# A list schedule that models the port pair of VectorE and GpSimd, and picks engines without a discount

## Chip, cores and metric

One Trainium2 chip, one core. The metric is the device time of one execution in microseconds (us); lower is better. In the profile PE is TensorE, DVE is VectorE, ACT is ScalarE, POOL is GpSimd, SP is the queue that issues the DMAs.

## What is computed

A two-layer decoder trunk over 1024 tokens of width 1024, in float32. Each layer is a residual step:

```python
h = rms_norm(x, ln_g[layer]); u = h @ w_in[layer]          # one wide projection
# even layer: latent attention | compressed + selected + window attention | memory attention
# odd layer:  attention over the 256 best keys of an index score | mLSTM (chunked) | memory attention
mix = concat([y1 * silu(gate1), y2 * silu(gate2), y_m * silu(gate_m)])
x = x + mix @ w_out[layer]
```

Every attention is scores, mask, softmax over the keys, and a weighted sum of the values, for 4 or 8 heads.

## The kernel before

The work is tiled by 128 rows (eight tiles of tokens). Products are made in halves: a float32 operand is split into a high half in 16 bits (a cast) and a low half (the operand minus its high half), and three matmuls take the place of one. So each weight page `wr` (128x1024) is multiplied by a gain in place, cast to the high part of `wl`, and the low part of `wl` is `wr` minus the high part. Likewise each page of exponentials `P` that goes through a DMA transpose is cast into `PS` and has its low half subtracted (`u_split`). `nm` is the negated row maximum of a score tile, to which a constant is added; `cf` is a factor per head; `ms` is a mean square whose root is taken on GpSimd by a power operation.

The program is not written in order. `Recorder.add` records each instruction with its dependencies and a price in ns (`cost_of`). `Recorder.places` gives each instruction a place by the segment it belongs to (the table `SEG`). `Recorder.order` is a greedy list schedule: of the engines T, V, S, G (TensorE, VectorE, ScalarE, GpSimd) and Q (the DMA queue) it takes, again and again, the one whose next instruction could start first by the prices and by `latency`, and issues it. What comes out is one fixed sequence for each engine; the semaphores follow from the data, and no planned time goes into the program.

Some instructions may run on more than one engine (`Recorder.flex`): casts and scalings made by `copy` on V or S, elementwise operations of two tensors made by `tt` and `sub` on V or G. `elsewhere` decides for those, with the alternatives' prices weighted by `PRICE`:

```python
fin = {x: max(te[x], ready(o, x), shared(o, x), room) + alt[3] * (1 + PRICE[x]) for x, alt in o.alts.items()}
return min(fin.values()) < fin[e]
```

`te` is when the engine ends what it was last given. `shared` keeps an engine off a tile or bank of PSUM that another engine still touches. The prices that matter here, for m elements in a partition: V, two tensors, 1.042 m + 69; V, one tensor in SBUF, 0.525 m + 65; G, two tensors, 1.886 m + 148 with a 16-bit result and 2.104 m + 148 with a 32-bit one; S, 0.8333 m + 94 from SBUF.

Of the kernel before, what the change touches and what calls it, by code (L numbers as in the profile page):

```python
# [14 lines left out]
OP = mybir.AluOpType  # L15
# [9 lines left out]
PRICE = {"V": 1.12, "S": 1.2, "G": -0.64}  # L25
BANKED = ("B",)
_BASE = np.zeros(8 << 20, np.uint8)
_BASE0 = _BASE.__array_interface__["data"][0]

class VTile:  # L30
    """a tile that gets its place when the first instruction that touches it is issued"""
# [18 lines left out]
class View:  # L50
    """a view of a VTile: shape and extent now, the access pattern when it is issued"""
# [60 lines left out]
    def box(self):  # L112
        """partition and byte extent (p0, p1, b0, b1)"""
# [30 lines left out]
class Op:  # L144
    __slots__ = ("eng", "alts", "deps", "users", "cost", "tiles", "key", "seg", "ldw", "idx", "ndep", "end", "where", "name", "real", "start", "banks")
# [12 lines left out]
class Recorder:  # L158
    """records instructions, orders them by a list schedule over the engines, and issues them"""
# [7 lines left out]
    @contextmanager  # L167
    def segment(self, name, t0, t1):
        """instructions recorded inside take their places in the program from t0 to t1"""
        old, self.seg = self.seg, self.segs.setdefault(name, [t0, t1, 0.0])  # L170
        yield
        self.seg = old

    def flex(self, *alts):
        """alternatives (engine, method, args, keywords) for one instruction; the schedule takes one"""
        o = self.add(*alts[0])
        for eng, meth, args, kw in alts[1:]:
            outs, ins = self.split(args, kw)
            o.alts[eng] = (meth, args, kw, cost_of(eng, meth, outs, ins, args, kw))
        return o  # L180
# [9 lines left out]
    def add(self, eng, meth, args, kw):  # L190
# [28 lines left out]
        o.alts = {eng: (meth, args, kw, o.cost)}  # L219
        o.ldw = 0.0 if eng != "Q" else max(1220.0, 395 + o.cost) if kw.get("transpose") else PLAIN  # L220
# [4 lines left out]
        o.key = self.seg[2]  # L225
        o.where = None
# [3 lines left out]
    # ---------------------------------------------------------------- list schedule  # L230
    def places(self):
        """the program: instructions by place, work of the tensor engine ahead of each, first and last place of each tile"""
# [3 lines left out]
        for o in ops:  # L236
            t0, t1, w = o.seg
            o.key = t0 + (t1 - t0) * o.key / max(w, 1e-9)
# [54 lines left out]
    def order(self, window=6183873, dma_window=39829):  # L293
# [28 lines left out]

        def shared(o, e):
            """when the engines that touched the tiles of o first, or its banks last, let engine e at them"""
            t = 0.0
            for v in o.tiles:
                if v in first and first[v][0] != e:
                    t = max(t, first[v][1] + latency(first[v][0], e))
# [6 lines left out]
        def elsewhere(p, e):  # L335
            """whether another engine would finish the instruction at p well before e would, the engines' time at its price"""
# [13 lines left out]
        def clock(st, cost):  # L350
            """time of an instruction of the tensor engine, whose clock halves after a window with little work"""
# [16 lines left out]
        def fits(v, p, now):  # L368
            """(time, first slot) of the best free place for a tile of the instruction at p, or None; a pair of banks is kept for the next
            tile that needs one"""  # L370
# [15 lines left out]
        def alloc(p, now):  # L386
            """earliest time for the tiles that the instruction at p brings up, or None"""
# [14 lines left out]
        while len(out) < n:  # L402
# [100 lines left out]
            else:  # L503
                o.end = te[e] = st + (clock(st, o.cost) if e == "T" else o.cost)
            changed = False
# [43 lines left out]

def cost_of(eng, meth, outs, ins, args, kw):  # L550
    """nanoseconds an engine is held"""
    if meth.startswith("dma"):
# [7 lines left out]
        return a.size * a.itemsize / (360.0 if run >= 512 else 180.0)  # L560
# [35 lines left out]
def latency(a, b):  # L596
    """from the end of an instruction on engine a to the start of one on engine b that needs it"""
# [69 lines left out]
class Trunk:  # L667
# [64 lines left out]
    def sub(self, out, a, b, scale=1.0, engs="VG"):  # L732
        """out = a * scale - b"""
# [21 lines left out]
    # ------------------------------------------------------------------ constants  # L755
# [27 lines left out]
    def setup_late(self):  # L783
# [30 lines left out]
        # gains of keys without rotation go to the queries; a power of two balances queries and keys  # L814
# [64 lines left out]
    def rope(self, u, C, Sn, a, b, out):  # L879
        """u, a, b, out: [128, h, d]; C, Sn: [128, d]"""  # L880
# [7 lines left out]
    def split_rows(self, u, name, k=2, dup=1, dt=H):  # L888
        """u: [128, h, d] fp32; [128, h, k, d]: hi, lo (k = 2), hi, lo, lo, hi (k = 4) or hi, hi, lo, lo (dup = 2)"""
# [20 lines left out]
    def turn(self, out, in_):  # L910
        """out [128, n, rows] = in_ [rows, 128 * n] transposed, 128 columns at a time"""
        self.Q.dma_start(out, in_, transpose=True)

    def flip(self, src, dt=H):
        """transposes split rows src (list of [128 or less, 128]) into one psum bank"""
# [8 lines left out]
    # ------------------------------------------------------------------ normalised, transposed, split rows  # L924
    def norm_T(self, xt, tag):
        """rows of xt over their root mean square, times 1024: halves hi and lo, transposed"""
# [14 lines left out]
    # ------------------------------------------------------------------ weights  # L941
    def load_w(self, parts, nk, gain=None, fuse=False):
        """parts: list of dram AP [nk*128, n]; last: list over k of (hi [128, n], lo [128, n]) of the rows times gain times a power of
        two, and [128, 2]: what takes their products with rows times 1024 back, and half of it"""
# [1484 lines left out]
```

## Time and profile before

| | |
|---|---|
| median of 3 runs | 1698.34 us |
| lowest, highest | 1695.55 us, 1702.73 us |
| span of the profiled execution | 1695.3 us |
| instructions | 30,499 |
| matmuls | 10,407 |
| mean granted clock of TensorE | 0.949 |

The profiled execution has no time of its own beside its span of 1695.3 us; the median of the timed runs is 3.0 us above that span. An engine's busy time counts an instruction from start to end, and that includes the time in which it stood still after its start.

### The profile page before, as it was taken

How to read it: one execution, taken by the hardware profiler on the slowest of the kernel's cores; microseconds unless marked ns; L12 is line 12 of the kernel's file. 1: busy time of each engine (PE TensorE's matmuls, PEld its weight loads, DVE VectorE, ACT ScalarE, POOL GpSimd, SP SyncE). 2: the span in 40 equal slices, each digit the busy share in tenths (PEclk: the TensorE clock that was granted, in tenths of full speed). 3: DMA queues.
4: the chain of work that ended last, by engine and by line, in shares of the span. 5: the costliest groups of instructions: out<-in, count | busy, mean ns of one | idle time of the engine just before them, and what ended most of it. 6: DMA issues, size and time to landing. Idle time of an engine off the chain costs nothing. (4 is left out here: it accounts for less than half of the span.)

```text
span 1695.3 us, 30499 instructions
## 1 busy us (share of the span) xinstructions
PE 1420.5 (84%) x10407; PEld 795.2 (47%) x10407; DVE 1494.5 (88%) x3574; ACT 937.2 (55%) x2282; POOL 967.6 (57%) x982
## 2 busy tenths in 40 slices
PE   4889978888788877868888798788996788999888
PEld 1334434445566654544555354333442345556454
DVE  8864699999988998898888989989999799999894
ACT  5521545345666675555664357697965544355541
POOL 3563479888756566566565653423148667645461
PEclk9899989999999999979999899999998788899999
DMA  9804512237577778867996240021242036579997
GB/s 280 212 22 107 190 50 87 89 102 150 110 130 128 169 154 232 199 118 162 219 226 144 57 139 15 16 91 32 85 131 67 30 75 164 141 173 200 236 220 171
DMA packets 441853, 225.52 MB, mean 133 GB/s; under 512 B 378080, under 2 KB 404320, under 8 KB 441696
## 3 DMA queue, kind: packets, MB, share of 16 engines
q1 hardware_dynamic: 441696, 223.57, 55.7%
q8 instruction: 81, 1.33, 0.3%
q14 instruction: 76, 0.62, 0.1%
HBM read 83.61 MB, written 46.66 MB: 77 GB/s over the span
## 5 line engine op out<-in xcount | busy, mean ns | idle before, releaser
L542 PE MATMUL psum<-wl,hT 128*128 128x512 f16 (+3 forms) x2880 | 707.8, 382 | 40.4 <-POOL wl L542 9.1
L542 PEld LDWEIGHTS <-hT 128*128 128x128 f16 x2880 | 286.4, 101 | 354.4 <-issue 91.1
L542 POOL TENSOR_TENSOR PS<-P,PS 128x512 f16<-128x512 f32 (+6 forms) x153 | 216.7, 1418 | 122.3 <-DVE PS L542 54.3
L542 PE MATMUL psum<-wl,oT 128*128 128x512 f16 x960 | 273.2, 384 | 9.8 <-DMA oT<-osp 2.4
L542 PEld LDWEIGHTS <-PT 128*128 128x128 f16 x3792 | 235.3, 102 | 93.9 <-DMA PT<-PS 35.0
L542 ACT ACTIVATE P<-psum,nm 128x256 f32<-128x256 f32 (+8 forms) x336 | 191.8, 580 | 135.8 <-POOL nm L542 45.6
L542 POOL TENSOR_TENSOR wl<-wr,wl 128x1024 f16<-128x1024 f32 (+4 forms) x77 | 180.2, 2347 | 118.1 <-DVE wl L542 70.7
L542 PE MATMUL psum<-nv,PT 128*128 128x64 f16 x1584 | 189.1, 195 | 22.1 <-DVE PT L542 11.4
L542 POOL TENSOR_TENSOR ms<-ms,nhalf 128x4 f32<-128x4 f32 (+3 forms) x105 | 121.5, 1165 | 132.9 <-DVE ms L542 115.1
L542 ACT ACTIVATE tkj<-tkj 128x512 bf16<-128x512 bf16 (+5 forms) x192 | 149.5, 780 | 73.4 <-DVE tkj L542 50.1
L542 DVE TENSOR_REDUCE nm<-psum 128x2 f32<-128x512 f32 (+8 forms) x216 | 162.5, 763 | 15.5 <-PE psum L542 14.8
L542 PEld LDWEIGHTS <-oT 128*128 128x128 f16 x960 | 93.9, 99 | 104.8 <-issue 12.6
L542 PE MATMUL psum<-cst,P 128*128 128x128 f32 x502 | 106.6, 300 | 21.4 <-ACT P L542 11.5
L542 PEld LDWEIGHTS <-qf 128*128 128x128 f16 x832 | 78.2, 100 | 64.1 <-issue 29.0
L542 ACT ACTIVATE PT<-psum 128x512 f16<-128x512 f32 (+3 forms) x160 | 76.7, 504 | 50.6 <-PE psum L542 43.0
L542 PE MATMUL psum<-nkst,qf 128*128 128x320 f16 (+5 forms) x384 | 92.2, 317 | 13.9 <-ACT P L542 8.6
L542 DVE CAST PS<-P 128x512 f16<-128x512 f32 (+6 forms) x139 | 86.1, 622 | 12.1 <-ACT P L542 5.6
L542 DVE TENSOR_TENSOR PT<-psum,PT 128x512 f16<-128x512 f32 (+3 forms) x160 | 87.8, 564 | 6.1 <-ACT PT L542 5.8
L542 PEld LDWEIGHTS psum<-cst,P 128*128 128x128 f32 x502 | 67.6, 145 | 46.0 <-ACT P L542 21.1
L542 PE MATMUL psum<-cvp,PT 128*128 128x64 f16 x864 | 76.5, 194 | 10.8 <-DMA PT<-PS 9.5
L542 ACT ACTIVATE wj<-wr 128x1024 bf16<-128x1024 f32 (+3 forms) x65 | 66.1, 1017 | 28.0 <-DMA wr<-even_w_in 19.6
L542 PE MATMUL psum<-vp,PT 128*128 128x64 f16 x864 | 70.3, 196 | 7.2 <-DMA PT<-PS 5.8
(499 smaller groups left out, 3161.9 us busy)
## 6 DMA issues: line engine op xcount, KB each, us to landing
wr<-even_w_in SPq DMA_DIRECT2D x20, 512.0 KB, 6.1
wr<-w_out SPq DMA_DIRECT2D x20, 512.0 KB, 5.1
wr<-odd_w_in SPq DMA_DIRECT2D x20, 512.0 KB, 5.3
gate<-gate_d SPq DMA_DIRECT2D x32, 256.0 KB, 4.3
gate_d<-gu SPq DMA_DIRECT2D x24, 256.0 KB, 2.2
qa_d<-mqT SPq DMA_DIRECT2D x16, 384.0 KB, 2.5
xt<-x SPq DMA_DIRECT2D x8, 512.0 KB, 9.1
x<-x SPq DMA_DIRECT2D x8, 512.0 KB, 5.0
```

The source lines that it names most:

```text
L542: r = getattr(engines[o.eng], meth)(*[res(a) for a in args], **{k: res(v) for k, v in kw.items()})
```

## The change

The prices `PRICE` become zero, so that `elsewhere` compares the plain finish times. Each price gets a fixed addition for its engine. `takes_ports` says which instructions hold the port pair that VectorE and GpSimd share, `order` notes when each engine lets it go, and `shared` keeps the other engine off until then. DMAs are priced by lower rates. `places` restores its inputs, so that it could be called twice; it is called once. Comments and docstrings go. `SEG`, the windows of `order`, `LAT` and everything that is computed stay as they are.

```diff
-PRICE = {"V": 1.12, "S": 1.2, "G": -0.64}
+PRICE = {"V": 0.0, "S": 0.0, "G": 0.0}
+EXTRA = {"V": 6.0, "S": 30.0, "G": 35.0, "T": 0.0, "Q": 0.0}
+FREED = {"V": 57.0, "G": 95.0}
...
     def flex(self, *alts):
...
             o.alts[eng] = (meth, args, kw, cost_of(eng, meth, outs, ins, args, kw))
+            o.lock[eng] = takes_ports(eng, meth, outs, ins, args, kw)
...
+        o.lock = {eng: takes_ports(eng, meth, outs, ins, args, kw)}
...
+        ports = {"V": 0.0, "G": 0.0}
+
         def shared(o, e):
             t = 0.0
+            if o.lock[e]:
+                t = ports["V" if e == "G" else "G"]
...
                 o.end = te[e] = st + (clock(st, o.cost) if e == "T" else o.cost)
+                if o.lock[e]:
+                    ports[e] = st + o.lock[e] * o.cost - FREED[e]
...
+def takes_ports(eng, meth, outs, ins, args, kw):
+
+    if eng == "G":
+        return 0.7 if kw.get("op") == OP.pow else 1.0
+    if eng != "V" or not ins or "accum_out" in kw and meth == "tensor_scalar":
+        return 0.0
+    psum = lambda v: v.t.tag in BANKED
+    if meth in ("tensor_tensor", "tensor_tensor_reduce", "scalar_tensor_tensor", "tensor_tensor_scan"):
+        two = [v for k, v in kw.items() if k in ("in0", "in1", "data0", "data1")]
+        return float(not any(psum(v) for v in two))
+    if meth in ("tensor_copy", "tensor_scalar"):
+        return float(not psum(ins[0]) and not psum(outs[0]) and np.prod(outs[0].arr.shape[1:]) > 1)
+    return 0.0
...
 def cost_of(eng, meth, outs, ins, args, kw):
+    return time_of(eng, meth, outs, ins, args, kw) + EXTRA[eng]
+
+
+def time_of(eng, meth, outs, ins, args, kw):
...
-        return a.size * a.itemsize / (360.0 if run >= 512 else 180.0)
+        return a.size * a.itemsize / (290.0 if run >= 512 else 150.0)
```

## Rows read from the trace of the kernel before

**Rows 1.** The page, its first part: busy time of each engine, share of the span, instructions.

```profile
PE 1420.5 (84%) x10407; PEld 795.2 (47%) x10407; DVE 1494.5 (88%) x3574; ACT 937.2 (55%) x2282; POOL 967.6 (57%) x982
```

**Rows 2.** Busy time of each engine in stretches of 100 us, and the sum over the whole span. The columns are the stretch, its length, then PE, PEld (weight loads), DVE, ACT and POOL with their instructions, granted clock, DMA share and GB/s.

```profile
300.00:400.00 100.00, 81.72 (x528) 46.04 (x526) 94.67 (x306) 46.12 (x156) 83.11 (x108) 0.95 0.43 109
...
1100.00:1200.00 100.00, 88.79 (x397) 40.05 (x395) 90.74 (x274) 86.20 (x210) 28.51 (x25) 0.97 0.24 78
...
1600.00:1695.00 95.00, 82.52 (x739) 45.39 (x739) 71.00 (x165) 32.33 (x70) 38.90 (x22) 0.98 0.84 199
sum 1695.00, PE 1420.53 PEld 795.17 DVE 1494.54 ACT 937.19 POOL 967.63; mean PE 83.56 PEld 46.77 DVE 87.91 ACT 55.13 POOL 56.92
```

**Rows 3.** Instructions in order of time near 104 us, on DVE and POOL: start, duration, engine, operation, tiles, shapes.

```profile
103.80 2.17 POOL L542 TENSOR_TENSOR wl<-wr,wl 128x1024 f16<-128x1024 f32 x1
104.02 2.10 DVE L542 CAST ks<-ku 128x256 f16<-128x256 f32 x1
...
107.25 0.29 DVE L542 CAST ks<-ku 128x256 f16<-128x256 f32 x1
```

**Rows 4.** The same near the end of the span, POOL alone.

```profile
1639.99 2.14 POOL L542 TENSOR_TENSOR PS<-P,PS 128x1024 f16<-128x1024 f32 x1 [2.37 <-DVE nm L542]
1644.79 2.14 POOL L542 TENSOR_TENSOR PS<-P,PS 128x1024 f16<-128x1024 f32 x1 [2.66 <-DVE PS L542]
```

**Rows 5.** The same stretch, DVE alone.

```profile
1639.90 0.73 DVE L542 SCALAR_TENSOR_TENSOR x<-psum,oe,x 128x512 f32<-128x512 f32 x1
1640.56 1.21 DVE L542 CUSTOM_DVE_ANT_0 smask<-psum,dmask 128x1024 f32<-128x1024 f32 x1
...
1642.14 0.47 DVE L542 TENSOR_SCALAR osp<-mixA,oe 128x512 f16<-128x512 f32 x1
...
1645.48 1.73 DVE L542 TENSOR_SCALAR osp<-mixA,oe 128x512 f16<-128x512 f32 x1
```

**Rows 6.** Instructions by tile, for the tiles `nm`, `PS`, `wl` and `wr`: engine, operation, count, then the shortest, the median and the longest duration in ns, first and last start, and the commonest shapes.

```profile
L542 DVE TENSOR_TENSOR nm<-nm,lnp x116: 123/155/1845, 372.6 to 1657.7; 128x1 f32<-128x1 f32 x67, 128x2 f32<-128x2 f32 x35, 128x4 f32<-128x4 f32 x14
L542 POOL TENSOR_TENSOR nm<-nm,lnp x100: 184/192/1227, 384.6 to 1652.6; 128x1 f32<-128x1 f32 x77, 128x2 f32<-128x2 f32 x13, 128x4 f32<-128x4 f32 x10
...
L542 POOL TENSOR_TENSOR PS<-P,PS x153: 663/1397/2552, 377.9 to 1661.8; 128x512 f16<-128x512 f32 x59, 128x640 f16<-128x640 f32 x29, 128x384 f16<-128x384 f32 x17, 128x768 f16<-128x768 f32 x14
L542 DVE CAST PS<-P x139: 280/484/2336, 394.1 to 1661.3; 128x512 f16<-128x512 f32 x50, 128x640 f16<-128x640 f32 x29, 128x384 f16<-128x384 f32 x16, 128x768 f16<-128x768 f32 x13
L542 ACT ACTIVATE PS<-P x21: 417/631/1048, 375.9 to 1594.2; 128x512 f16<-128x512 f32 x12, 128x256 f16<-128x256 f32 x2, 128x384 f16<-128x384 f32 x2, 128x896 f16<-128x896 f32 x2
L542 DVE TENSOR_TENSOR PS<-P,PS x7: 410/655/2148, 381.9 to 1521.8; 128x512 f16<-128x512 f32 x3, 128x256 f16<-128x256 f32 x2, 128x640 f16<-128x640 f32 x1, 128x384 f16<-128x384 f32 x1
...
L542 POOL TENSOR_TENSOR wl<-wr,wl x77: 1544/2243/4865, 20.5 to 1628.0; 128x1024 f16<-128x1024 f32 x67, 128x864 f16<-128x864 f32 x4, 128x832 f16<-128x832 f32 x3, 128x768 f16<-128x768 f32 x2
L542 DVE CAST wl<-wr x68: 413/681/2612, 19.8 to 1621.8; 128x1024 f16<-128x1024 f32 x60, 128x832 f16<-128x832 f32 x3, 128x864 f16<-128x864 f32 x3, 128x512 f16<-128x512 f32 x1
L542 ACT ACTIVATE wl<-wr x20: 619/1052/1057, 74.2 to 1622.5; 128x1024 f16<-128x1024 f32 x16, 128x768 f16<-128x768 f32 x1, 128x832 f16<-128x832 f32 x1, 128x512 f16<-128x512 f32 x1
L542 DVE TENSOR_TENSOR wl<-wr,wl x11: 679/1214/3134, 26.5 to 1623.0; 128x1024 f16<-128x1024 f32 x9, 128x832 f16<-128x832 f32 x1, 128x512 f16<-128x512 f32 x1
...
L542 DVE TENSOR_SCALAR wr<-wr,wgs x78: 408/478/2381, 18.6 to 1335.1; 128x512 f32<-128x512 f32 x65, 128x432 f32<-128x432 f32 x5, 128x384 f32<-128x384 f32 x4, 128x416 f32<-128x416 f32 x4
...
L542 ACT ACTIVATE wr<-wr,wgs x56: 627/711/752, 18.6 to 1334.0; 128x512 f32<-128x512 f32 x49, 128x416 f32<-128x416 f32 x4, 128x432 f32<-128x432 f32 x3
```

**Rows 7.** Groups of instructions by engine and tile, the costliest first: count, busy time in us, mean duration in ns, idle time before them and what ended it.

```profile
L542 POOL TENSOR_TENSOR PS<-P,PS 128x512 f16<-128x512 f32 (+6 forms) x153 | 216.7, 1418 | 122.3 <-DVE PS L542 54.3 <-DVE nm L542 20.6 <-issue 15.8
...
L542 POOL TENSOR_TENSOR wl<-wr,wl 128x1024 f16<-128x1024 f32 (+4 forms) x77 | 180.2, 2347 | 118.1 <-DVE wl L542 70.7 <-DVE ms L542 19.7 <-issue 12.1
L542 DVE TENSOR_REDUCE nm<-psum 128x2 f32<-128x512 f32 (+8 forms) x216 | 162.5, 763 | 15.5 <-PE psum L542 14.8 <-ACT P L542 0.4
...
L542 POOL TENSOR_TENSOR ms<-ms,nhalf 128x4 f32<-128x4 f32 (+3 forms) x105 | 121.5, 1165 | 132.9 <-DVE ms L542 115.1 <-DVE dss L542 7.0 <-DVE oss L542 3.9
...
L542 DVE TENSOR_TENSOR PT<-psum,PT 128x512 f16<-128x512 f32 (+3 forms) x160 | 87.8, 564 | 6.1 <-ACT PT L542 5.8
L542 DVE CAST PS<-P 128x512 f16<-128x512 f32 (+6 forms) x139 | 86.1, 622 | 12.1 <-ACT P L542 5.6 <-DMA PT<-PS 3.8 <-ACT oj L542 2.0
...
L542 DVE TENSOR_SCALAR wr<-wr,wgs 128x512 f32<-128x512 f32 (+3 forms) x78 | 58.5, 778 | 0.1
L542 DVE CAST wl<-wr 128x1024 f16<-128x1024 f32 (+4 forms) x68 | 57.7, 855 | 4.8 <-PE psum L542 4.6 <-issue 0.2
...
L542 DVE TENSOR_TENSOR nm<-nm,lnp 128x1 f32<-128x1 f32 (+2 forms) x116 | 47.2, 407 | 0.3
...
L542 DVE CUSTOM_DVE_ANT_0 smask<-psum,dmask 128x384 f32<-128x384 f32 (+5 forms) x48 | 41.9, 880 | 1.4 <-PE psum L542 1.2
...
L542 POOL TENSOR_TENSOR nm<-nm,lnp 128x1 f32<-128x1 f32 (+2 forms) x100 | 28.5, 286 | 82.6 <-DVE nm L542 69.3 <-DVE cf L542 6.8 <-DVE wsb L542 5.1
...
L542 POOL TENSOR_TENSOR mqms<-mqms,nhalf 128x8 f32<-128x8 f32 x16 | 27.4, 1714 | 7.1 <-DVE mqms L542 7.0
...
L542 POOL TENSOR_TENSOR x<-x,ot 128x512 f32<-128x512 f32 x16 | 22.1, 1381 | 2.3 <-ACT ot L542 2.3
...
L542 DVE TENSOR_TENSOR wl<-wr,wl 128x1024 f16<-128x1024 f32 (+2 forms) x11 | 19.4, 1768 | 0.0
```

More of the change, by code (lines that the diff above doesn't have):

```diff
@@ L144 @@
 class Op:
-    __slots__ = ("eng", "alts", "deps", "users", "cost", "tiles", "key", "seg", "ldw", "idx", "ndep", "end", "where", "name", "real", "start", "banks")
+    __slots__ = ("eng", "lock", "key0", "home", "alts", "deps", "users", "cost", "tiles", "key", "seg", "ldw", "idx", "ndep", "end", "where", "name", "real", "start", "banks")
 class Engine:
@@ L225, in add @@
         o.key = self.seg[2]
+        o.key0, o.home = o.key, (eng, o.cost)
         o.where = None
@@ L236, in places @@
         for o in ops:
+            o.users = []
+        for o in ops:
             t0, t1, w = o.seg
-            o.key = t0 + (t1 - t0) * o.key / max(w, 1e-9)
+            o.key = t0 + (t1 - t0) * o.key0 / max(w, 1e-9)
+            o.eng, o.cost = o.home
             for d in o.deps:
```

## The prediction

> **What bounds the kernel now.** I read the busy times first. VectorE is busy for 1494.5 of 1695.3 us, TensorE for 1420.5, GpSimd for 967.6 and ScalarE for 937.2 [rows 1]. Two engines are close to the span, so the second view is the one by stretches: from 300 to 400 us VectorE is busy 94.67 of 100 us and TensorE 81.72; from 1100 to 1200 us 90.74 and 88.79; only in the last 95 us does VectorE fall to 71 and TensorE lead [rows 2]. VectorE sets the pace through most of the span, with TensorE close behind. Its idle time over the whole span is 1695.3 - 1494.5 = 200.8 us.
>
> The third view asks what that busy time is. In order of time near 104 us, a cast of a 128x256 tile takes 2.10 us on VectorE while GpSimd runs a 2.17 us subtraction that began 0.22 us before it; both end within 0.15 us of each other. The same cast takes 0.29 us three microseconds later [rows 3]. Near the end a scaling of `mixA` into `osp` takes 1.73 us and ends 0.28 us after a 2.14 us subtraction on GpSimd, and 0.47 us without one [rows 4, 5]. But in the 2.14 us of GpSimd that start at 1639.99, VectorE runs two instructions with one input in PSUM, of 0.73 and 1.21 us, one behind the other [rows 4, 5]. So part of VectorE's busy time is standing still behind GpSimd, and it hits instructions whose inputs are all in SBUF.
>
> The Trainium skill says this as a rule ("SBUF — State Buffer", section "Who interferes with whom"): the pair of ports is held for a whole instruction, and whoever comes second waits. The trace agrees: 2.10 us against 0.29.
>
> How much is it? By tile, the medians and the means lie far apart where this happens [rows 6, 7]: `nm` 155 and 407 ns (116 instructions, 29.2 us in excess of the median), the cast into `PS` 484 and 622 (139, 19.2 us), the cast into `wl` 681 and 855 (68, 11.8 us), the scaling of `wr` 478 and 778 (78, 23.4 us), the subtraction into `wl` 1214 and 1768 (11, 6.1 us). That is 89.7 of the groups' 268.9 us, a third. From VectorE's 1494.5 us I take off what reads PSUM, 162.5 + 87.8 + 41.9 us in the three largest groups [rows 7], and for the smaller ones and for reductions another 190 us (my estimate); some 1010 us may be blocked. A third would be 337 us. I use 310, since among the five are the shortest instructions, for which one block weighs most. VectorE without blocks then has 1185 us of work, and a microsecond of GpSimd costs VectorE 310 / 967.6 = 0.32 us.
>
> **The change, part by part.** Only the sequences of the engines change and who runs the flexible instructions; nothing is computed otherwise, no wait is written in, and no DMA is added.
>
> *Discount gone, VectorE against GpSimd.* By the planner's old prices a low half of 512 elements cost V (1.042 x 512 + 69) x 2.12 = 1277 and G (1.886 x 512 + 148) x 0.36 = 401: GpSimd took it unless it was 876 ns late. The trace shows the result: 153 low halves of `PS` on GpSimd and 7 on VectorE, 77 of `wl` and 11 [rows 6]. The new prices are 609 and 1149, for `wl` (1024) 1142 and 2114: VectorE takes it unless it, or the ports, are 540 or 972 ns late. VectorE is late by that much only behind a long instruction that leaves the ports free. I therefore move all 77 of `wl`, half of the low halves of `PS`, half of `nm`, and half of the rest. On GpSimd `ms` (121.5), `mqms` (27.4), `x` (22.1 us) and tables and copies (25, estimate) are fixed, together 196; the rest is 967.6 - 196 - 216.7 - 180.2 - 28.5 = 346 us [rows 1, 7]. GpSimd loses 180 + 108 + 14 + 173 = 475 us and keeps 492. VectorE gains 77 x 1.214 = 93, 76 x 0.655 = 50, 50 x 0.155 = 8, and 173 x 1214/2243 = 94 us [rows 6]: together 245.
>
> *VectorE against ScalarE.* A copy of 512 had weighted prices of 708 and 1145, so ScalarE took it if VectorE was 437 ns late; now 340 and 551, a gap of 211, and a VectorE that waits for the ports counts as late. The three large groups of copies hold 202.3 us on VectorE (285 instructions) [rows 7]. I move a quarter: VectorE loses 50 us, ScalarE gains 71 x 0.75 = 53 us by the medians of 0.63 to 1.05 [rows 6], on an engine busy 937 us of 1695 [rows 1]; idle time of ScalarE hides it. Without that cover, from 1100 to 1200 us where ScalarE is busy 86 of 100 us [rows 2], it would cost up to a tenth of it.
>
> *The lock.* It changes order only. In the plan VectorE takes a reader of PSUM while GpSimd works. On the chip each engine goes through its list as its semaphores allow, and nothing keeps the planned moments. Bounds for what VectorE still stands still: 0 if the plan holds to the microsecond, and 492 x 0.32 = 157 us if the order carries nothing over. I take half, 79 us, because GpSimd's inputs mostly come from VectorE, so that the two are tied to each other: of the 122.3 us that GpSimd waited ahead of `PS`, 54.3 ended with VectorE's cast [rows 7].
>
> The Trainium skill has a sentence against this part, in the same section of that page: "Issue order, not op shape, decides who blocks." By it a plan that fixes no moments gives 157 and not 79, and the sum below would be 41 us above the present time. It is the third case below.
>
> *EXTRA, DMA rates, `places`.* They shift planned moments; the work stays. The DMA rates may let loads be planned a little later and never faster; they share the SP queue as before. I cost them at nothing. What hides it is the lead with which loads are issued; if that is gone, the waits on transfers come back by a few microseconds each.
>
> *Sum.* VectorE: 1494.5 - 310 + 245 - 50 + 79 = 1458.5, which is 36 us less. With its idle time unchanged at 200.8, the span is 1659 us; the median of the runs is 3.0 us above the profiled span, so 1662. Shorter latencies (a low half of `PS` 0.655 against 1.397 us [rows 6]) take perhaps 2 us of idle: 1660.
>
> **The rivals.** *Contention is gone almost whole, and TensorE bounds.* VectorE falls to 1380, and the span cannot follow: TensorE has 1420.5 us of work, and if it keeps 170 of its 275 us of idle, the time is 1590. For it: the blocks are a fifth of VectorE's time. Against it: the order must hold on the chip.
>
> *The lock does nothing on the chip.* 157 us of blocks: VectorE at 1494.5 - 310 + 245 - 50 + 157 = 1536; if the copies to ScalarE and the better order of long waits each give back some 20 us, the time is about 1700, no change.
>
> *VectorE is overfilled.* This is the other side. The discount made the scarce engine dear. Without it each decision looks at one instruction and takes VectorE, which is nearly twice as fast, and not at the queue behind. By the numbers above, an instruction of GpSimd costs VectorE 0.32 of its time in blocks, and 1214/2243 = 0.54 if VectorE does it itself. If three quarters of GpSimd's 771 us of flexible work move, VectorE gains 578 x 0.54 = 312; GpSimd keeps 390, with half of 125 us of blocks: 1494.5 - 310 + 312 - 50 + 62 = 1508, and with whole blocks 1571, which gives 1712 to 1775. I price it at 1735. It decides from the point where more than 0.6 of the flexible work moves while less than half of the blocks go away. For it: `SEG` and the windows stay as they were while the prices they go with change. Against it: VectorE counts as late while it runs its many PSUM readers, and GpSimd then takes work.
>
> **How the numbers follow.** The forecast of 1660 has a chance of 0.46, with 1620 to 1690 its own range; contention gone, 1590, 0.14; no change 0.14; VectorE overfilled, 1735, 0.26. Half a percent, 8 us, is about what a measurement of this kernel tells from no change. So faster 0.60, same 0.14, slower 0.26. The range goes from 1590 to 1740: it takes in both ends of the blocks (1583 and 1740, with idle time unchanged) but for a little, and leaves out what is faster than TensorE's case or slower than the overfilled one.
>
> **What would show it.** Right: GpSimd's busy time falls to about 490 us; nearly all low halves of `wl` are on VectorE; the mean of `nm` on VectorE comes down from 407 towards 155 ns, and the mean of the scaling of `wr` from 778 towards 478; ScalarE's busy time rises by some 50 us; VectorE is busy for about 1460 us. Wrong: means that stay a third above their medians say that the lock does not reach the chip; VectorE above 1500 us with longer gaps on TensorE says that it is overfilled; low halves that stay on GpSimd say that the engines are chosen otherwise than I think. The prediction would also fail if TensorE, not VectorE, waits longer at the seams between the stages, which no term here counts.

## The result

The changed kernel takes 1616.36 us (median of 4 runs, 1611.16 to 1623.3) against 1696.94 for the kernel before, a ratio of 0.953 with a 95% interval of 0.950 to 0.956. The forecast was 1660: the direction was right, but the fall that was forecast, 38 us, is less than half of the 81 us measured.

The page of the changed kernel, first part (busy us, share of the span of 1613.7 us, instructions):

```profile
PE 1416.9 (88%) x10407; PEld 805.0 (50%) x10407; DVE 1397.4 (87%) x3836; ACT 1051.8 (65%) x2492; POOL 411.4 (25%) x512
```

Against [rows 1] TensorE's busy time stands (1420.5 and 1416.9 us). VectorE loses 97.1 us, GpSimd loses 556.2, and ScalarE gains 114.6. TensorE's idle time went from 1695.3 - 1420.5 = 274.8 to 196.8 us; VectorE's from 200.8 to 216.3.

The same by stretches (columns as in [rows 2]):

```profile
300.00:400.00 100.00, 76.96 (x615) 47.69 (x614) 96.95 (x328) 67.81 (x231) 52.65 (x66) 0.88 0.67 147
...
900.00:1000.00 100.00, 96.37 (x475) 49.46 (x474) 93.89 (x234) 83.51 (x170) 10.04 (x16) 0.98 0.22 69
1000.00:1100.00 100.00, 100.00 (x475) 46.90 (x473) 87.83 (x308) 94.63 (x229) 7.41 (x7) 1.00 0.25 81
...
1500.00:1600.00 100.00, 87.54 (x778) 48.79 (x777) 81.56 (x187) 45.05 (x89) 12.27 (x10) 0.92 0.88 200
...
sum 1613.00, PE 1416.92 PEld 804.96 DVE 1397.38 ACT 1051.78 POOL 411.41; mean PE 83.35 PEld 47.35 DVE 82.20 ACT 61.87 POOL 24.20
```

GpSimd, at 83 of 100 us from 300 to 400 before, is at 53 there and at 7 to 12 in the other stretches shown. From 1000 to 1100 us TensorE is busy without a gap and ScalarE for 95 us, so in that stretch VectorE is no longer what sets the pace.

By tile (shortest, median, longest ns), as in [rows 6]:

```profile
L557 POOL TENSOR_TENSOR nm<-nm,lnp x110: 183/192/1787, 347.1 to 1560.5; 128x1 f32<-128x1 f32 x73, 128x2 f32<-128x2 f32 x23, 128x4 f32<-128x4 f32 x14
L557 DVE TENSOR_TENSOR nm<-nm,lnp x106: 117/153/1223, 338.3 to 1564.7; 128x1 f32<-128x1 f32 x71, 128x2 f32<-128x2 f32 x25, 128x4 f32<-128x4 f32 x10
...
L557 DVE TENSOR_TENSOR PS<-P,PS x142: 381/692/1485, 344.8 to 1576.7; 128x512 f16<-128x512 f32 x55, 128x640 f16<-128x640 f32 x25, 128x384 f16<-128x384 f32 x15, 128x768 f16<-128x768 f32 x14
L557 DVE CAST PS<-P x101: 266/479/1475, 367.8 to 1576.0; 128x512 f16<-128x512 f32 x34, 128x640 f16<-128x640 f32 x24, 128x384 f16<-128x384 f32 x11, 128x1024 f16<-128x1024 f32 x11
L557 ACT ACTIVATE PS<-P x59: 417/631/1084, 341.6 to 1550.2; 128x512 f16<-128x512 f32 x28, 128x384 f16<-128x384 f32 x7, 128x896 f16<-128x896 f32 x7, 128x640 f16<-128x640 f32 x6
L557 POOL TENSOR_TENSOR PS<-P,PS x18: 672/1372/2132, 433.3 to 1447.6; 128x512 f16<-128x512 f32 x7, 128x640 f16<-128x640 f32 x5, 128x384 f16<-128x384 f32 x3, 128x256 f16<-128x256 f32 x2
...
L557 DVE TENSOR_TENSOR wl<-wr,wl x82: 687/1216/1270, 21.4 to 1539.9; 128x1024 f16<-128x1024 f32 x70, 128x832 f16<-128x832 f32 x4, 128x864 f16<-128x864 f32 x4, 128x512 f16<-128x512 f32 x2
L557 ACT ACTIVATE wl<-wr x51: 619/1049/1115, 44.1 to 1538.9; 128x1024 f16<-128x1024 f32 x45, 128x832 f16<-128x832 f32 x3, 128x864 f16<-128x864 f32 x2, 128x512 f16<-128x512 f32 x1
L557 DVE CAST wl<-wr x37: 422/686/1736, 20.2 to 1533.2; 128x1024 f16<-128x1024 f32 x31, 128x768 f16<-128x768 f32 x2, 128x864 f16<-128x864 f32 x2, 128x832 f16<-128x832 f32 x1
...
L557 POOL TENSOR_TENSOR wl<-wr,wl x6: 2125/2254/3052, 558.8 to 1540.0; 128x1024 f16<-128x1024 f32 x6
...
L557 ACT ACTIVATE wr<-wr,wgs x91: 607/710/766, 19.4 to 1224.5; 128x512 f32<-128x512 f32 x77, 128x416 f32<-128x416 f32 x6, 128x432 f32<-128x432 f32 x6, 128x384 f32<-128x384 f32 x2
...
L557 DVE TENSOR_SCALAR wr<-wr,wgs x43: 411/477/488, 19.4 to 1214.5; 128x512 f32<-128x512 f32 x37, 128x384 f32<-128x384 f32 x2, 128x416 f32<-128x416 f32 x2, 128x432 f32<-128x432 f32 x2
```

142 low halves of `PS` and 82 of `wl` are on VectorE now, 18 and 6 on GpSimd: the picture of before, turned over. Of the copies into `wl` ScalarE has 51 (20 before), of the scalings of `wr` 91 (56). The longest scaling of `wr` on VectorE falls from 2381 to 488 ns, and the longest low half of `wl` from 3134 to 1270.

By groups (count, busy us, mean ns), as in [rows 7]:

```profile
L557 POOL TENSOR_TENSOR ms<-ms,nhalf 128x4 f32<-128x4 f32 (+3 forms) x105 | 122.7, 1175 | 490.0 <-DVE ms L557 417.1 <-DVE nm L557 42.5 <-DVE oe L557 20.1
...
L557 DVE TENSOR_TENSOR wl<-wr,wl 128x1024 f16<-128x1024 f32 (+4 forms) x82 | 96.8, 1182 | 0.3 <-ACT wl L557 0.2
...
L557 DVE CAST PS<-P 128x512 f16<-128x512 f32 (+6 forms) x101 | 50.4, 502 | 5.9 <-ACT P L557 4.0 <-PE psum L557 1.1 <-DMA PT<-PS 0.6
...
L557 DVE CAST wl<-wr 128x1024 f16<-128x1024 f32 (+4 forms) x37 | 26.0, 708 | 1.4 <-ACT wr L557 1.0 <-PE psum L557 0.4
...
L557 DVE TENSOR_TENSOR nm<-nm,lnp 128x1 f32<-128x1 f32 (+2 forms) x106 | 23.4, 226 | 0.2
...
L557 DVE TENSOR_SCALAR wr<-wr,wgs 128x512 f32<-128x512 f32 (+3 forms) x43 | 19.4, 470 | 0.1
```

The mean of `nm` on VectorE fell from 407 to 226 ns with nearly the same median (155 and 153), that of `wr` from 778 to 470, that of the cast into `PS` from 622 to 502. The excess of mean over median in the five groups of the forecast was a third of their busy time; it is 11 us of 216 now, 5% (106 x 0.073, 101 x 0.023, 37 x 0.022 us, the other two nothing).

For the experiments I counted blocks over the whole trace: VectorE's instructions sorted by operation, shape, and whether they read or write PSUM, and of each one that takes over 15% and 40 ns longer than the lower quartile of its kind, the excess. That gives 310 us before (460 instructions) and 42 us (110) in the changed kernel, so 0.32 and 0.10 us per us of GpSimd. "Blocked" below is this number.

Two things in the traces say that this excess is standing still behind GpSimd. Of the 814 instructions of VectorE in the kernel before that read or write PSUM, none exceeds its kind by that much, though GpSimd is busy for 57% of the span [rows 1]. And the excess goes with what GpSimd does. A count with slightly wider bounds (316 us in all), split by the instruction of GpSimd that overlaps longest, puts 119 us beside the low halves of `wl` (0.66 us per us of GpSimd), 61 us beside those of `PS` (0.28), and under 1 us beside the 122 us of roots `ms`. The rate of 0.32 is a mean over work of very different cost.

What TensorE waited for, before (us in total, times, longest):

```profile
PE psum L542 <- ACT P L542: 37.0, 42, 4.8
PE psum L542 <- DVE PT L542: 32.3, 43, 1.8
PE psum L542 <- DVE wst L542: 31.2, 4, 16.4
PE psum L542 <- DMA PT<-PS: 24.5, 20, 2.8
PE psum L542 <- POOL wl L542: 13.7, 12, 4.4
...
PE psum L542 <- DVE wl L542: 8.2, 8, 1.8
```

and in the changed kernel:

```profile
PE psum L557 <- DMA PT<-PS: 43.9, 33, 4.4
PE psum L557 <- ACT P L557: 26.2, 28, 3.1
PE psum L557 <- DVE wl L557: 18.9, 6, 11.2
PE psum L557 <- DVE wst L557: 14.9, 4, 10.6
PE psum L557 <- DVE PT L557: 10.8, 19, 1.3
```

The waits on VectorE's `PT` and on the sums of the weights `wst` shrink from 32.3 and 31.2 us to 10.8 and 14.9. The wait on GpSimd's `wl` is gone, but with the low halves that on VectorE's `wl` grew from 8.2 to 18.9. The wait on the DMA transpose of `PS` grew from 24.5 to 43.9. Added up over all rows of this view, the waits that VectorE ended fell from 144 to 92 us, ScalarE's from 73 to 40 and GpSimd's from 16 to none, while those that a DMA ended rose from 35 to 59.

### The profile page after: what moved, and what is told of

It reads as the page before. It is cut to its first block, busy times and chain, and to the rows that moved or that the text cites. A ratio compares the mean times of both kernels' runs of the same rounds, so it can differ in the third digit from the quotient of the medians.

```text
span 1613.7 us, 30256 instructions
## 1 busy us (share of the span) xinstructions
PE 1416.9 (88%) x10407; PEld 805.0 (50%) x10407; DVE 1397.4 (87%) x3836; ACT 1051.8 (65%) x2492; POOL 411.4 (25%) x512
## 5 line engine op out<-in xcount | busy, mean ns | idle before, releaser
L557 PE MATMUL psum<-wl,hT 128*128 128x512 f16 (+3 forms) x2880 | 664.4, 373 | 26.6 <-DVE wl L557 12.0
L557 PEld LDWEIGHTS <-PT 128*128 128x128 f16 x3792 | 220.3, 102 | 96.6 <-DMA PT<-PS 57.4
L557 ACT ACTIVATE P<-psum,nm 128x256 f32<-128x256 f32 (+7 forms) x336 | 191.8, 581 | 79.1 <-POOL nm L557 30.6
L557 PE MATMUL psum<-nv,PT 128*128 128x64 f16 x1584 | 178.7, 197 | 24.7 <-DMA PT<-PS 18.4
L557 DVE TENSOR_REDUCE nm<-psum 128x2 f32<-128x512 f32 (+7 forms) x216 | 161.9, 765 | 21.3 <-PE psum L557 20.8
L557 ACT ACTIVATE tkj<-tkj 128x640 bf16<-128x640 bf16 (+5 forms) x192 | 149.7, 782 | 36.3 <-DVE tkj L557 34.0
L557 DVE TENSOR_TENSOR PS<-P,PS 128x512 f16<-128x512 f32 (+6 forms) x142 | 115.0, 815 | 0.0
L557 ACT ACTIVATE wj<-wr 128x1024 bf16<-128x1024 f32 (+4 forms) x77 | 78.0, 1015 | 32.7 <-DMA wr<-even_w_in 16.2
L557 DVE TENSOR_TENSOR wl<-wr,wl 128x1024 f16<-128x1024 f32 (+4 forms) x82 | 96.8, 1182 | 0.3 <-ACT wl L557 0.2
L557 POOL TENSOR_TENSOR nm<-nm,lnp 128x1 f32<-128x1 f32 (+2 forms) x110 | 31.8, 291 | 160.6 <-DVE nm L557 148.9
```

The source lines that it names most:

```text
L557: r = getattr(engines[o.eng], meth)(*[res(a) for a in args], **{k: res(v) for k, v in kw.items()})
```

## The experiments

Each run is compared with the kernel before, run beside it; that median was 1696.9 to 1700.1 us.

| run | what | median us | ratio to before, 95% | blocked us | GpSimd busy |
|---|---|---|---|---|---|
| | before | 1696.9 | 1 | 310 | 967.6 |
| | changed | 1616.4 | 0.950 to 0.956 | 42 | 411.4 |
| e3 | old discount, no lock | 1746.2 | 1.024 to 1.034 | 308 | 963.7 |
| e1 | old discount, lock | 1709.2 | 1.005 to 1.009 | 182 | 1110.4 |
| e2 | no discount, no lock | 1631.3 | 0.957 to 0.965 | 137 | 656.9 |
| e9 | all on VectorE | 1634.5 | 0.957 to 0.967 | 7 | 200.6 |
| e4 | engines fixed, lock | 1627.7 | 0.951 to 0.966 | 32 | 401.8 |
| e5 | engines fixed, no lock | 1634.4 | 0.957 to 0.969 | 66 | 411.4 |
| e6 | old engines, no lock | 1727.8 | 1.010 to 1.026 | 282 | 959.3 |
| e7 | old engines, lock | 1701.5 | 0.999 to 1.004 | 175 | 948.7 |
| g3 | before, no discount | 1659.7 | 0.972 to 0.981 | 135 | 646.4 |
| g1 | before, EXTRA | 1703.4 | 1.001 to 1.005 | 293 | 958.6 |
| g2 | before, DMA rates | 1751.3 | 1.026 to 1.037 | 308 | 961.4 |
| e8 | changed, old DMA rates | 1612.9 | 0.947 to 0.954 | 44 | 416.6 |
| p1 | before, latency 205 | 1707.9 | 1.003 to 1.008 | 304 | 962.8 |
| a1 | changed, latency 205 | 1608.4 | 0.943 to 0.951 | 44 | 409.0 |
| f1 | halves of `PS` on GpSimd | 1593.6 | 0.933 to 0.944 | 55 | 552.3 |
| f2 | halves of `wl` on GpSimd | 1632.0 | 0.955 to 0.964 | 129 | 575.4 |
| h1 | e1, halves of `wl` on VectorE | 1661.5 | 0.974 to 0.984 | 101 | 948.1 |
| h2 | f1, halves of `wl` on VectorE | 1589.7 | 0.933 to 0.941 | 59 | 547.1 |

### Discount and lock, each alone

e1 takes back the discount, e2 the lock, e3 both; EXTRA and the DMA rates stay.

```diff
# e1 and e3
-PRICE = {"V": 0.0, "S": 0.0, "G": 0.0}
+PRICE = {"V": 1.12, "S": 1.2, "G": -0.64}
# e2 and e3
 def takes_ports(eng, meth, outs, ins, args, kw):
+    return 0.0
```

> The changed kernel with the old discount (PRICE 1.12, 1.2, -0.64) and with the lock. Theory A, the lock's order reaches the chip: GpSimd keeps most of its work (above 750 us), but VectorE stands still for much less than 0.3 us per us of GpSimd, and the time is below 1670 us. Theory B, the gain comes from less work on GpSimd and the lock only moves planned moments: VectorE is blocked at the old rate of about 0.3, and the time is 1690 or more.

> The changed kernel with takes_ports returning 0 everywhere: no discount, no lock. Theory A: GpSimd's work falls to about 400 to 550 us, but each us of it still blocks VectorE for about 0.3 us (130 to 160 us in all, against some 40 in the changed kernel), so the time is 1650 to 1690 us. Theory B: the same as the changed kernel, 1616 us within 10.

> The changed kernel with the old discount and without the lock, so that only EXTRA and the DMA rates are left of the change. Both theories A and B: as before, 1697 us within 15. A third theory C, the gain comes from planned moments that fit the chip better (EXTRA, DMA rates): below 1660 us.

The pages of e1, e2 and e3, first part:

```profile
PE 1431.0 (84%) x10407; PEld 811.1 (48%) x10407; DVE 1278.3 (75%) x3092; ACT 1003.2 (59%) x2392; POOL 1110.4 (65%) x1356
```

```profile
PE 1417.8 (87%) x10407; PEld 801.3 (49%) x10407; DVE 1425.4 (87%) x3621; ACT 1017.2 (62%) x2425; POOL 656.9 (40%) x792
```

```profile
PE 1444.5 (83%) x10407; PEld 810.6 (47%) x10407; DVE 1506.0 (86%) x3574; ACT 926.5 (53%) x2267; POOL 963.7 (55%) x997
```

Between these four runs taking the discount away is worth 1746.2 - 1631.3 = 114.9 us without the lock and 92.8 with it; the lock is worth 37.0 us with the discount and 14.9 without it. Both theories are half right. A is right on the blocks: the lock brings them from 0.32 to 0.16 us per us of GpSimd at the old discount, and from 0.21 to 0.10 at none. It is wrong on the time: e1 was to fall below 1670 and came to 1709. B is right that less work on GpSimd is most of the gain; e2 came 15 us above the changed kernel, neither at 1616 nor at 1650. Without the discount GpSimd has 656.9 us of work, and 411.4 once the lock tells the planner what an instruction there waits for: the lock also moves work. e3 met no theory: 1746 against 1697 within 15 (A and B) or below 1660 (C); its 48 us are taken up under the scatter.

The row to stop at is e1's. VectorE is busy for 1278.3 us, 119 less than in the changed kernel, and the kernel is slower than before. So a sum that takes VectorE's busy time plus a constant for the span does not hold from one assignment to another.

### All on VectorE

```diff
-    def tt(self, out, in0, in1, op, engs="VG"):
+    def tt(self, out, in0, in1, op, engs="V"):
 # the same for sub, LOENG and NMENG
```

> The changed kernel with every instruction that could run on VectorE or GpSimd put on VectorE. The overfilling rival: GpSimd keeps about 200 us of fixed work, VectorE gains some 80 to 100 us over the changed kernel's 1397, and the time is 1680 us or more. If VectorE is not the bound any more after the change: within 15 of 1616.

```profile
PE 1419.2 (87%) x10407; PEld 800.3 (49%) x10407; DVE 1436.1 (88%) x4186; ACT 1049.1 (64%) x2477; POOL 200.6 (12%) x177
```

The overfilling rival falls. With nothing flexible left on GpSimd VectorE is busy for 1436.1 us, 39 more than in the changed kernel, with 7 us of blocks, and the time is 1634.5: 18 above the changed kernel and 64 below the kernel before.

### The order alone, engines fixed

The planner runs twice; the first plan only fixes the engines.

```diff
     def finish(self):
+        self.rec.locking = True      # False in e6 and e7, which have the old discount
+        self.rec.order()
+        for o in self.rec.ops:
+            o.alts = {o.eng: o.alts[o.eng]}
+        self.rec.locking = True      # e4 and e7; False in e5 and e6
         self.rec.issue(self.real, self.rec.order())
...
-            if o.lock[e]:
+            if self.locking and o.lock[e]:
```

> The changed kernel planned twice: the first plan only fixes which engine each flexible instruction runs on, the second orders them anew with the lock on. A control for the next two: every theory expects the changed kernel's 1616 us within 15, GpSimd at about 411 us of work, VectorE blocked for about 0.1 us per us of GpSimd.

> The same assignment to engines as in the control, ordered in the second plan without the lock. Theory A, the order keeps the port users apart on the chip: GpSimd still at about 411 us, but VectorE is blocked at 0.2 to 0.3 us per us of it (80 to 125 us against some 40), and the time rises by 10 to 40 us over the control. Theory B, only who runs what counts: the time and the blocked time are those of the control.

> The old discount and no lock, planned twice in the same way, lock off in both: the control for the next one. Every theory expects 1746 us within 20, GpSimd at about 964 us, VectorE blocked at 0.32 us per us of it.

> The assignment of the control just before (old discount, GpSimd at about 964 us), ordered in the second plan with the lock on. Theory A: VectorE blocked at 0.1 to 0.2 us per us of GpSimd, that is 100 to 190 us in place of 308. If VectorE's busy time sets the time, the time falls by as much as VectorE's busy time; if what counts is how long a result takes through GpSimd, it falls by less than a third of that. Theory B: blocked as before, and the time of the control.

The pages of e4, e5, e6 and e7, first part:

```profile
PE 1423.4 (88%) x10407; PEld 806.1 (50%) x10407; DVE 1389.2 (85%) x3836; ACT 1048.7 (65%) x2492; POOL 401.8 (25%) x512
```

```profile
PE 1422.7 (87%) x10407; PEld 806.4 (49%) x10407; DVE 1420.5 (87%) x3836; ACT 1045.0 (64%) x2490; POOL 411.4 (25%) x512
```

```profile
PE 1447.4 (84%) x10407; PEld 808.8 (47%) x10407; DVE 1485.3 (86%) x3574; ACT 923.5 (53%) x2267; POOL 959.3 (55%) x997
```

```profile
PE 1429.5 (84%) x10407; PEld 807.9 (48%) x10407; DVE 1376.2 (81%) x3574; ACT 926.4 (54%) x2269; POOL 948.7 (56%) x997
```

Within each pair the counts of instructions on VectorE and GpSimd are the same (3836 and 512; 3574 and 997), and the order alone differs. With the lock blocks fall from 282 to 175 us (e6, e7) and from 66 to 32 (e5, e4), and VectorE's busy time with them, by 109.1 and 31.3 us. So the planned order does reach the chip, though no wait is written into the program. But of VectorE's 109.1 us the time gives back 26.4 (1727.8 to 1701.5), and of 31.3 us 6.7, whose intervals overlap. e5 was also blocked less, and e4 gained less on it, than Theory A expected (66 us against 80 to 125, 6.7 us against 10 to 40).

The 26.4 us are less than a third of the 109.1, as Theory A has it for the case that a result's way through GpSimd counts. That this is the reason is not shown, and f1 below speaks against it. What the waits of TensorE show, e6 and then e7:

```profile
PE psum L557 <- DMA PT<-PS: 27.8, 23, 3.2
```

```profile
PE psum L557 <- DMA PT<-PS: 54.2, 40, 5.3
```

Over all rows of the view the waits that VectorE ended fell from 138 to 92 us, and those that a DMA ended rose from 38 to 77. TensorE waited less for VectorE and more for the transposes; why these came late is open.

### Where GpSimd's work should be

f1 leaves the low halves of `PS` to GpSimd alone, f2 those of `wl`; about the same work each.

```diff
# f1
-LOENG = "GV"
+LOENG = "G"
# f2, in load_w
-            self.sub(flat(lo), flat(r3), flat(hi))
+            self.sub(flat(lo), flat(r3), flat(hi), engs="G")
```

> The changed kernel with the low halves of PS (the exponentials that go through a DMA transpose) on GpSimd alone; the planner knows it and has the lock. VectorE loses about 142 x 0.69 = 98 us of work. If VectorE's busy time sets the time, it falls below 1600 us. If it is the time that a result takes through GpSimd (1.4 us against 0.69, on the way from the scores to the transpose and the next matmul), it rises to 1630 to 1670 us although VectorE has less to do.

> The changed kernel with the low halves of the weights wl on GpSimd alone; VectorE loses as much as in the run before, 82 x 1.18 = 97 us. Weights are loaded ahead of their use. If the way through GpSimd counts, this one costs little: 1600 to 1630 us. If VectorE's busy time counts, it falls below 1600 us just as the run before.

The pages of f1 and f2, first part:

```profile
PE 1409.4 (89%) x10407; PEld 801.1 (50%) x10407; DVE 1337.6 (84%) x3769; ACT 1046.9 (66%) x2486; POOL 552.3 (35%) x585
```

```profile
PE 1403.2 (86%) x10407; PEld 797.3 (49%) x10407; DVE 1413.0 (87%) x3794; ACT 1048.2 (64%) x2462; POOL 575.4 (35%) x582
```

If the way through GpSimd counted, f1 would be slow and f2 cheap; if VectorE's work counted, both would be fast. Neither holds: f1 is faster than the changed kernel by 23 us, f2 slower by 16. GpSimd is busier by 141 us in f1 and by 164 in f2, but in f1 blocks grow by 13 us, in f2 by 87, and so VectorE, which gives up as much work in both, falls to 1337.6 us in one and rises to 1413.0 in the other. In order of time near the start, f2 on GpSimd and VectorE (a row with x4 or x2 merges that many instructions; start, duration):

```profile
20.10 10.20 POOL L557 TENSOR_TENSOR wl<-wr,wl 128x1024 f16<-128x1024 f32 x4 [0.67 <-DVE wl L557]
...
40.24 0.48 DVE L557 TENSOR_SCALAR wr<-wr,wgs 128x512 f32<-128x512 f32 x1
...
45.01 4.39 POOL L557 TENSOR_TENSOR wl<-wr,wl 128x1024 f16<-128x1024 f32 x2 [11.69 <-ACT wl L557]
45.04 2.37 DVE L557 TENSOR_SCALAR wr<-wr,wgs 128x512 f32<-128x512 f32 x1
```

Weights come in bursts: four low halves stand one behind the other on GpSimd for 10.20 us, and a scaling of `wr` on VectorE takes 2.37 us under the first of the next two, 0.48 at 40.24, where GpSimd is idle. The casts and scalings of the same burst are among those VectorE instructions that GpSimd blocks: the longest scaling of `wr` takes 2374 ns in f2, 488 in the changed kernel. Low halves of `PS` mostly come singly, with readers of PSUM beside them, as the one at 1639.99 did [rows 4, 5]. The traces bear this out. In f2 85 us of blocks lie beside the 196 us of low halves of `wl`, 0.43 per us; in f1 27 us beside the 227 us of those of `PS`, 0.12 per us. Instructions with an operand in PSUM run on VectorE for 26% of the former time and for 62% of the latter. Without its blocks VectorE has 1283 us of work in f1 and 1284 in f2. That the blocks make up all of the 38 us between the two is not shown.

h1 makes the same test from the other end: e1's discount and lock, with the low halves of `wl` on VectorE alone. h2 puts f1 and this together.

```diff
# h1 and h2, in load_w
-            self.sub(flat(lo), flat(r3), flat(hi))
+            self.sub(flat(lo), flat(r3), flat(hi), engs="V")
```

> The changed kernel with the old discount and the lock (1709 us, GpSimd 1110 us, VectorE 1278), but with the low halves of the weights, the longest instructions of GpSimd (88 of 2.2 us), on VectorE alone. VectorE gains about 88 x 1.2 = 106 us. Theory D, with the discount short results such as the roots ms stand in line behind long instructions of GpSimd, and that is what costs: the time falls below 1690 us although VectorE has more to do, and the roots start nearer to their inputs. Theory V, VectorE's busy time sets the time: it rises above 1725 us.

> The changed kernel with the low halves of PS on GpSimd alone, as in the fastest run so far (1594 us), and the low halves of the weights on VectorE alone. By the two runs that moved one of them: 1585 to 1605 us, GpSimd at about 550 us, VectorE blocked for about 50. If the fastest run was a good draw: 1605 to 1625 us.

The pages of h1 and h2, first part:

```profile
PE 1429.6 (86%) x10407; PEld 808.2 (49%) x10407; DVE 1271.2 (76%) x3159; ACT 1016.2 (61%) x2416; POOL 948.1 (57%) x1265
```

```profile
PE 1398.4 (88%) x10407; PEld 797.8 (50%) x10407; DVE 1350.3 (85%) x3781; ACT 1046.8 (66%) x2483; POOL 547.1 (34%) x576
```

h1 is 48 us faster than e1 while VectorE's busy time stands (1278.3 and 1271.2): the 88 low halves that it took over are paid by 81 us fewer blocks (82 us of e1's lay beside them) and by other work that moved. Theory V falls here. Theory D, that short results stand in line on GpSimd, was to show in the roots `ms`. The views by tile of `ms` say how long GpSimd sat idle before a root until VectorE had its input, and at how many of the 105 roots; most of the others had another instruction of GpSimd ahead of them. Before, changed, e1 and h1, in this order:

```profile
  DVE ms L542: 115.1, 41
```

```profile
  DVE ms L557: 417.1, 65
```

```profile
  DVE ms L557: 115.8, 26
```

```profile
  DVE ms L557: 206.4, 34
```

GpSimd was idle and waiting for VectorE at 41 of the 105 roots before, at 65 in the changed kernel, at 26 in e1 and 34 in h1. The line is longest where GpSimd has most to do. But from e1 to h1 it shortened by little, and 48 us went; that the line is the cause of them is not shown.

h2 is the fastest of all: 1589.7 us, 0.937 (0.933 to 0.941) of the kernel before, and below the changed kernel by 27 us. It is not to be told from f1.

### New prices and scatter

g1, g2 and g3 give the kernel before one part each: EXTRA, the DMA rates, no discount. e8 takes the DMA rates out of the changed kernel. p1 and a1 move one number without a reason to be better, to see what another draw of the sequences does.

```diff
# p1 on the kernel before, a1 on the changed one
-    return LAT.get((a, b), 200.0)
+    return LAT.get((a, b), 205.0)
```

> The kernel before with the three discounts set to zero and nothing else: no lock, no EXTRA, the old DMA rates. If the discount is the main part of the change: 1616 to 1650 us. If the gain needs the lock or the new prices: 1680 us or more.

> The kernel before with EXTRA alone (6, 30 and 35 ns on the prices of VectorE, ScalarE and GpSimd). With the old discount EXTRA and the DMA rates together cost 48 us (1746 against 1698). If EXTRA is the cause: 1735 us or more. If it is the DMA rates: within 12 of 1698.

> The kernel before with the new DMA rates alone. If they are the cause of the 48 us: 1735 us or more. If it is EXTRA: within 12 of 1698. If neither alone gives it, the 48 us are the scatter of sequences for segments that were fitted to one of them.

> The changed kernel with the old DMA rates. With the old discount the new rates alone cost 53 us (1751 against 1698). If they are bad for the sequences as such: the changed kernel gets faster without them, below 1595 us. If the 53 us belong to the discounted sequences alone: 1600 to 1635 us. If the new rates fit the new prices: 1640 us or more.

> The kernel before with one number of the planner moved by a little (the latency between engines, 205 for 200 ns), which changes the sequences but has no reason to be better or worse. If the sequences before were an uncommonly good draw for the fixed segments: 1715 us or more, towards the 1746 of the run with the old discount, no lock and the new prices. If not: 1697 within 10.

> The changed kernel with the planner's latency between engines at 205 for 200 ns: another draw of the sequences. If the changed kernel's 1616 us are typical of its planner: within 12 of it. If it was a good draw: 1635 us or more, near the run without the lock, so that the lock's 15 us would lie within the scatter.

No discount, alone, gives 1659.7 against 1698.5 beside it: 39 us, about half of the whole gain, and between the two expectations. EXTRA alone is within 7 us of before. The new DMA rates cost 54 us in the kernel before, as much as e3's loss, and do nothing in the changed kernel (1612.9 and 1616.4). Without the discount and the lock, EXTRA and the rates together go the other way, 1659.7 to 1631.3. A part whose sign hangs on the rest has no price of its own; I take these differences for what another set of sequences can do.

Of the 54 us the trace of g2 shows a part. Its page, first part, and the longest stretch in which its clock was low:

```profile
PE 1455.9 (83%) x10407; PEld 815.1 (47%) x10407; DVE 1491.9 (85%) x3553; ACT 939.3 (54%) x2294; POOL 961.4 (55%) x991
```

```profile
1472.00:1517.00 45.00, 43.36 (x132) 28.07 (x131) 30.21 (x79) 12.79 (x34) 17.29 (x11) 0.51 0.17 44
```

Between the profiled spans (1695.3 and 1749.5 us) TensorE's busy time takes 35.4 us and its idle time 18.8. Its granted clock has two levels, 1.2 and 2.4 GHz, and its mean fell from 0.949 to 0.926. TensorE was busy at the lower level for 136 us before and for 206 in g2; 70 us more at half the clock lose 35 us, an estimate, and that is the growth of its busy time. In the stretch shown the clock was at the lower level though TensorE was busy for 43 of 45 us, and for 12 of the 12 us ahead of it. So by this estimate about two thirds of the 54 us lie in the clock; why it was granted less with these sequences is open.

How far do sequences scatter? The 5 ns on the latency moved the kernel before by 9 us up and the changed one by 8 us down; planning twice moved e3 by 18 us (e6) and the changed kernel by 11 (e4). The sequences with the discount and no lock (before, p1, g1, e6, e3, g2) take 1697 to 1751 us, those of the change (a1, e8, changed, e4) 1608 to 1628: the gain of the whole change is clear of the scatter. With no discount and an order without the lock they take 1631 to 1660 (e2, e5, g3), with the discount and the lock 1701 and 1709 (e7, e1). So taking the discount away is clear of the scatter too, with the lock and without it. What the lock is worth in time is not: with the discount the two ranges overlap, without it they lie 3 us apart. The fall of the blocks in all four pairs is. f1 and h2 lie 15 and 19 us below a1, the fastest of the change's sequences.

## Why the prediction was wrong

**What bounds.** That a fifth of VectorE's busy time was standing still behind GpSimd was right: 310 us by the rows that I had, 310 by the count over the trace. That the two agree to the microsecond is luck: the rows gave 337, and 310 was a choice. All runs with the discount and no lock (e3, e6, g1, g2, p1) give 282 to 308 by that count.

**Discount.** The low halves moved as told for `wl` (6 left of 77) and more than told for `PS` (18 left of 153, half expected). `nm` went against the forecast: 110 on GpSimd after 100, not 50. GpSimd came to 411 us, not 492.

**The sum.** VectorE was to come to 1458.5 us and came to 1397.4; its idle time was to stay at 200.8 and was 216.3. Two terms were mis-sized. Copies: a quarter was to move and 50 us with it. In fact 104 of 285 moved, and 12 of the sums of squares `wj`: by their medians 38 x 0.479 + 31 x 0.686 + 35 x 0.477 + 12 x 1.216 = 71 us off VectorE, and ScalarE gained 115 us, not 53. The quarter had no source beside the prices. Without the lock ScalarE already gained 80 us (e2) and 93 (g3), so the smaller gap between the prices alone moved more than a quarter; with the lock, by which a VectorE that waits for the ports counts as late, it is 35 us more than in e2. The 50 us were also a quarter of busy times that still held blocks; by the medians a quarter is 38.

Blocks: 79 us forecast, 42 measured. Here the step that failed is the flat rate of 0.32 us per us of GpSimd, kept for whatever work stays there. The work that left was the dear one (`wl`, 0.66) and the roots, which stayed, block next to nothing: with the change's engines and no lock the blocks are 66 us (e5), not the 157 of the forecast's upper bound. That the lock then takes half of them away (66 to 32, e5 and e4) is what was forecast. The two terms make 21 + 37 = 58 of the 61 us by which VectorE was missed.

What VectorE took over from GpSimd is then 1397.4 - 1494.5 + 310 - 42 + 71 = 242 us, against 245 in the forecast. This is a remainder, and its agreement is luck: without blocks the low halves of `PS` brought VectorE 107 us by the traces (50 forecast) and those of `wl` 83 (93), so the rest brought some 52 where 102 were forecast.

**The step under the sum.** "With its idle time unchanged" was met by 16 us here and is still not a law. e7 and e6 differ in order alone, and 109.1 us less on VectorE gave 26.4. e1 has 216 us less than the kernel before and is slower. h1 and e1 have the same busy time and differ by 48 us. From the kernel before to the changed one TensorE's idle time has 78.0 of the 81.6 us, so there busy time of VectorE counts as far as a wait of TensorE ends with it. That is no law either: between e6 and e7 TensorE's busy time has 17.9 of the 31.4 us by which the profiled spans differ. I read the stretches for the engine that is busiest and did not read what TensorE's 275 us of idle were made of.

**The lock.** The rival that it does nothing on the chip is wrong for the blocks. What the plan changes is the issue order of two queues, and with the engines fixed that alone took 38% off them (282 to 175 us). The sentence of the Trainium skill weighed in the prediction ("SBUF — State Buffer", "Who interferes with whom": issue order decides who blocks) agrees with these runs; the prediction read it against the lock, and it speaks for it.

**The other rivals.** TensorE as the bound at 1590 was nearer to the time than the forecast (26 us against 44), and f1 and h2 reach it (1593.6 and 1589.7, with TensorE idle for 1591.9 - 1409.4 = 182.5 and 188.4 us, 170 in the rival). VectorE overfilled fell with e9. I had priced a scarce VectorE by its busy time, and of that a large part was blocks that go away with the work on GpSimd.

## What to carry to other kernels

Before a busy engine is taken for the bound, compare mean and median of its groups: blocks behind another engine show as means far above medians, and what is freed there comes back in time only where the pacing engine's waits end with it. A helper engine that is half as fast and shares ports is worth using for work that comes singly beside instructions that don't need the ports (f1), not for bursts whose other half needs them (f2). Price a block by what the helper runs, not by a mean rate. When a planner's prices change, run a few draws with an idle number moved, to know which differences are the plan's and which the draw's, and compare the clock that TensorE was granted.

## What the runs showed of the hardware

An order chosen without any wait keeps two engines off each other's ports to a good part: at the same assignment, 0.29 us of blocks per us of GpSimd became 0.18 (e6, e7), and 0.16 became 0.08 (e5, e4). An addition of at most four elements a partition on VectorE, 155 ns at the median, took up to 1845 ns behind GpSimd, and up to 1223 with the lock and without the discount. Not every instruction of GpSimd blocks VectorE. In the kernel before 165 instructions of VectorE, of kinds that are blocked elsewhere in the trace, began while a root `ms` ran, over 150 ns ahead of its end; 4 of them were blocked, and all took 0.9 us together more than the lower quartiles of their kinds. Of the 81 that began so under a low half of `wl` 66 were blocked, and the excess was 106 us. `takes_ports` holds the ports for 0.7 of a root all the same, so the plan there keeps VectorE from work that would hardly have been blocked.
